# One layer's last weight pair: the sum of two weight tiles made by an accumulating DMA from GpSimd's queue instead of a VectorE add

## The chip, the cores and the metric

The kernel runs on one core of one Trainium2 chip. The metric is the device time of one execution in microseconds (us). A profiled execution also has a span, from its first to its last instruction, and a granted TensorE clock; both are given below.

## The reference

The program is a trunk of two layers over 512 tokens of width 2048, in float32. Each layer normalises its input, projects it once into all heads' columns, runs two groups of heads (a gated linear attention and a chunked attention), joins what they give, projects it once more, normalises that and adds it to the residual stream.

```python
def hybrid_layer(x, w_in, w_out, g_pre, g_post, ...):
    h = rmsnorm(x, g_pre)
    z = h @ w_in
    ...
    y = jnp.concatenate([o_gla, o_att], axis=-1) @ w_out
    return x + rmsnorm(y, g_post)

def reference(x, w_in, w_out, ...):
    h = x
    for l in range(DEPTH):
        h = hybrid_layer(h, w_in[l], w_out[l], ...)
    return h
```

The change lies in `... @ w_out`, in the half of its columns that the kernel computes last.

## The kernel before

**Precision.** Every float32 operand is split into a rounded part and a rest (ScalarE casts `wh`, VectorE subtracts to get `wl`), and a product is three matmuls: `wh` twice and `wl` once.

**Pairs.** Weight blocks are 512 columns wide. Most of them are taken in pairs by `fast_gemm`, which makes the eight block products of a 2x2 block multiplication from seven, P1 to P7, of sums and differences of weight blocks (this file makes them from loaded tiles as it goes) and of token blocks (made earlier, kept in DRAM, loaded again as `sa`). Each product has four steps c = 0 to 3, a step loads one or two weight tiles of 128 x 1024 (512 KB), and feeds 12 matmuls. A pair's products are listed in a fixed order: the last pair of a layer, `W23` (the last 1024 columns of `w_out`), has an order of its own, `PROD_END`:

```python
PROD_END = order("10 11 50 12 51 13 52 53 60 61 30 62 31 63 32 33 20 21 22 23 70 71 72 73 40 41 42 43")
```

"72" is step c = 2 of P7. So in the last pair the four steps of P2 come first, then the four of P7, and then the four of P4, after which the layer is over. `w_consume` takes the finished products: it adds two partial results on VectorE (`combine`, L318, into `t`), squares and scales them (L1086 on ScalarE, L1087 on VectorE).

**One job of the stream.** `Job.load` issues the DMAs on SyncE's queue (`fetch`, L140), `Job.high` makes the tile that is to be multiplied and its cast `wh` (L182, ScalarE), `Job.low` its rest `wl` (L186, VectorE). `ahead` keeps five loads, four highs and three lows in front of the job that is being multiplied (L356). Tiles live in rings: four buffers for `raw`, four for `H`, four for `wh`, three for `wl`. A DMA into a `raw` tile waits until the last reader of that buffer is done.

**P7 of the last pair.** It needs the sum of two tiles of the second weight block, rows `c + 4` and rows `c`. Here `load` fetches both, into two `raw` buffers, and `high` adds the second to the first on VectorE (L176 and L177), before the cast. So four steps of a layer take eight `raw` loads and four adds of 128 x 1024. In all other pairs P7 is a difference of `H` and one loaded tile (L179).

**What runs beside it.** Tasks are fed in between the products. In the last pair these are `finish_token` (L1098 to L1115: L1100 sums squares, L402 is a power on GpSimd that makes the factor, L1112 adds the residual on VectorE, then a store from GpSimd's queue) and, in the first layer, `prep_half` for the second layer: squares of the new rows (L415, ScalarE), their scaling (L455, VectorE), transposes on TensorE (L465), which ScalarE brings out of PSUM (L475) and splits with VectorE (L105 and L106, into tiles `a`, `g8` and others). The next layer's first product, L282, takes those. Its first two token tiles need the first half of `prep_half`; its last two need the second half, the tile `g8` first.

**Order.** The instruction order on each engine is made by a scheduler that runs with a timeline of its own when the kernel is built. Each engine then works through its list in order. In the last layer P4's last three steps are held back (`lag`), and after the last matmul come the last token tiles' sums, scaling and stores.

Of the kernel before, what the change touches and what calls it, by code (L numbers as in the profile page):

```python
# [11 lines left out]
ALU = mybir.AluOpType  # L12
# [21 lines left out]
def hybrid_trunk(  # L34
# [12 lines left out]
    nc = tc.nc  # L47
# [16 lines left out]
    def nm(s):  # L64
        serial[0] += 1
        return f"{s}_{serial[0]}"
# [4 lines left out]
    def rtile(tag, shape=(2, W), dtype=F32, bufs=4):  # L71
        return ring.tile([P] + list(shape), dtype, tag=tag, name=nm(tag), bufs=bufs)
# [28 lines left out]
    def flat(t):  # L101
        return t.bitcast(F32).rearrange("p a b -> p (a b)")
# [22 lines left out]
    W23 = (NB_IN + 2, NB_IN + 3)  # L125
# [8 lines left out]
    class Job:  # L134
# [8 lines left out]
        def load(self):  # L143
            k, c, p, b0, b1 = self.kind, self.c, self.pair, self.b0, self.b1
            end = b0 == W23[0]
            top, bottom = (c + 4, c) if end else (c, c + 4)
            if k == "std":
                self.raw = self.fetch(rtile("raw"), b0, c)
            elif k == "P1":
                p["H", c] = self.fetch(rtile("H"), b0, top)  # L150
            elif k == "P5":
                p["r", c] = self.fetch(rtile("raw"), b1, top)
            elif k == "P6":
                p["r", c] = self.fetch(rtile("raw"), b1, bottom)
            elif k == "P7" and end:
                p["r", c] = self.fetch(rtile("raw"), b1, top)
                p["r2", c] = self.fetch(rtile("raw"), b1, bottom)
            elif k == "P7":
                p["r", c] = self.fetch(rtile("raw"), b0, top)
            elif k == "P2":  # L160
                p["r", c] = self.fetch(rtile("raw"), b0, bottom)
            src = (so_d if end else sa_d)[self.l].get((LEFT.get(k), c))
            if src is not None:
                self.a = rtile("sa", (2, 512), F32R)
                nc.sync.dma_start(flat(self.a), src)

        def high(self):
            k, c, p = self.kind, self.c, self.pair
            if k == "std":
                src = self.raw  # L170
            else:
                h, r = p["H", c], p.get(("r", c))
                src = h if k in ("P1", "P5", "P6", "P4") else r
                if k in ("P5", "P6"):
                    nc.vector.tensor_tensor(out=h, in0=h, in1=r, op=ALU.add)  # L175
                elif k == "P7" and ("r2", c) in p:  # L176
                    nc.vector.tensor_tensor(out=r, in0=r, in1=p["r2", c], op=ALU.add)  # L177
                elif k == "P7":
                    nc.vector.tensor_tensor(out=r, in0=h, in1=r, op=ALU.subtract)  # L179
            self.src = src  # L180
            self.wh = rtile("wh", dtype=F32R)
            last_cast[0] = nc.scalar.copy(self.wh, src).ins  # L182
# [1029 lines left out]
```

## Time and profile before

| | |
|---|---|
| median of 3 runs | 1685.46 us (1684.21 to 1686.59) |
| the profiled execution's own time | 1684.26 us |
| its span | 1682.2 us |
| mean granted TensorE clock | 0.995 |
| PE busy | 1640.6 us, 98% |
| DVE busy | 1208.0 us, 72% |
| ACT busy | 873.8 us, 52% |
| POOL busy | 158.0 us, 9% |

PE is TensorE, DVE VectorE, ACT ScalarE, POOL GpSimd, SP SyncE; L12 is line 12 of the kernel. A group of the profile is written as line, engine, operation, the tile written, an arrow, the tiles read. Busy time is a sum over the whole span; the two places of the change (P7 of layer 0 from 813 us, of layer 1 from 1642 us) are some 17 us long each, so they hardly show in it, and have to be looked at in windows.

### The profile page before, as it was taken

Reading aid. Unit: us, or ns where it says so; the run is one execution under the profiler, and the core shown is the slowest. Engines: PE = TensorE matmul, PEld = TensorE weight load, DVE = VectorE, ACT = ScalarE, POOL = GpSimd, SP = SyncE. Lnnn points to the kernel's source line nnn. Section 1 sums busy time; section 2 is a strip of 40 time slices with the busy share of each in tenths; the row PEclk is TensorE's granted clock in tenths of the full one; section 3 lists DMA queues with packets and bytes.
Section 4 is the critical chain, followed back from the end, with each engine's and each line's share of the span. In section 5 each row is a group of like instructions: output and inputs, shape, how many; then the busy total and the mean of one; then the engine's idle time right before and its main releaser. Section 6 shows DMA issues by size and latency. Waiting matters only on the chain.

```text
span 1682.2 us, 24940 instructions
## 1 busy us (share of the span) xinstructions
PE 1640.6 (98%) x9090; PEld 1401.0 (83%) x9090; DVE 1208.0 (72%) x1563; ACT 873.8 (52%) x1460; POOL 158.0 (9%) x256
## 2 busy tenths in 40 slices
PE   7999999999999999999999999999999999999996
PEld 5888889999988887788778878899999888777884
DVE  5846767686876876568887567677777768764787
ACT  8634544456665554335684345444556655443443
POOL 0210100001100001210132000000001001012101
PEclk9999999999999999999999999999999999999998
DMA  7987987867858797589779788868587687865993
GB/s 255 368 300 232 345 273 251 278 223 254 300 175 302 241 354 253 174 316 322 253 251 364 248 291 288 326 210 305 174 309 255 206 284 256 335 218 193 351 342 146
DMA packets 143002, 455.04 MB, mean 271 GB/s; under 512 B 15444, under 2 KB 32212, under 8 KB 142880
## 3 DMA queue, kind: packets, MB, share of 16 engines
q1 hardware_dynamic: 119984, 373.76, 65.1%
q0 software_dynamic: 22176, 78.41, 12.0%
q8 instruction: 72, 1.18, 0.3%
q10 hardware_dynamic: 720, 1.28, 0.2%
q14 instruction: 50, 0.41, 0.1%
HBM read 381.28 MB, written 72.11 MB: 270 GB/s over the span
## 4 chain that ended last, share of the span: by engine, by line
PE 85%; issue 4%; DVE 4%; DMA 4%; POOL 1%; ACT 1%; SPq 0%; DVEq 0%; POOLq 0%; ACTq 0%
PE mm L356 40%; PE mm L346 18%; PE mm L282 16%; DMA raw<-in_w_dram 2%; PE ax L766 2%; DVE wl L186 1%; PE ax L356 1%; PE ax L920 1%; PE ax L954 1%; PE ax L604 1%; PE ax L749 1%; DMA sa<-S 1%; POOL sm L402 1%; PE ax L730 1%; PE ax L728 1%
## 5 line engine op out<-in xcount | busy, mean ns | idle before, releaser
L356 PE MATMUL mm<-wh,sa 128*128 128x512 f32 x1536 | 495.0, 394 | 3.1 <-DMA sa<-S 1.6
L182 ACT CAST wh<-raw 128x1024 fp32r<-128x1024 f32 x248 | 261.6, 1058 | 277.7 <-PE mm L356 84.6
L186 DVE TENSOR_TENSOR wl<-raw,wh 128x1024 fp32r<-128x1024 f32 x248 | 302.1, 1221 | 107.1 <-PE mm L356 37.0
L356 PEld LDWEIGHTS mm<-wh,sa 128*128 128x128 f32 x1536 | 289.6, 189 | 67.4 <-ACT wh L182 4.5
L182 ACT CAST wh<-H 128x1024 fp32r<-128x1024 f32 x224 | 234.2, 1051 | 196.6 <-PE mm L356 101.3
L186 DVE TENSOR_TENSOR wl<-H,wh 128x1024 fp32r<-128x1024 f32 x224 | 272.9, 1222 | 88.2 <-PE mm L356 37.9
L356 PE MATMUL mm<-wl,sa 128*128 128x512 f32 x768 | 301.2, 392 | 5.7 <-DVE wl L186 5.7
L346 PE MATMUL mm<-sa,wh 128*128 128x256 f32 x1280 | 236.5, 285 | 0.0
L346 PEld LDWEIGHTS mm<-sa,wh 128*128 128x128 f32 x1280 | 199.5, 191 | 0.1
L356 PE MATMUL mm<-wh,a 128*128 128x512 f32 x576 | 189.1, 393 | 1.9 <-DVE t L318 1.9
L346 PE MATMUL mm<-sa,wl 128*128 128x256 f32 x640 | 181.4, 284 | 0.6 <-DVE wl L186 0.6
L356 PEld LDWEIGHTS mm<-wl,sa 128*128 128x128 f32 x768 | 144.9, 189 | 35.6 <-DVE wl L186 6.7
L282 PE MATMUL mm<-wh,a 128*128 128x512 f32 x512 | 169.4, 395 | 4.0 <-ACT a L105 2.2
L175 DVE TENSOR_TENSOR H<-H,raw 128x1024 f32<-128x1024 f32 x112 | 136.3, 1222 | 9.5 <-DMA raw<-in_w_dram 8.0
L356 PEld LDWEIGHTS mm<-wh,a 128*128 128x128 f32 x576 | 107.9, 188 | 24.9 <-DVE t L318 2.2
L346 PEld LDWEIGHTS mm<-sa,wl 128*128 128x128 f32 x640 | 122.5, 191 | 0.9 <-DVE wl L186 0.8
L282 PEld LDWEIGHTS mm<-wh,a 128*128 128x128 f32 x512 | 95.9, 188 | 26.8 <-ACT a L105 3.0
L402 POOL TENSOR_TENSOR sm<-sm,mhalf 128x2 f32<-128x2 f32 (+2 forms) x44 | 51.1, 1162 | 698.1 <-DVE sm L776 469.7
L356 PE MATMUL mm<-wl,a 128*128 128x512 f32 x288 | 112.9, 392 | 0.0
L179 DVE TENSOR_TENSOR raw<-H,raw 128x1024 f32<-128x1024 f32 x48 | 58.8, 1225 | 62.4 <-DMA raw<-in_w_dram 62.3
L282 PE MATMUL mm<-wl,a 128*128 128x512 f32 x256 | 100.4, 392 | 0.1
L346 PE MATMUL mm<-a,wh 128*128 128x256 f32 x512 | 95.1, 285 | 0.0
(193 smaller groups left out, 2348.2 us busy)
## 6 DMA issues: line engine op xcount, KB each, us to landing
raw<-in_w_dram SPq DMA_DIRECT2D x312, 512.0 KB, 5.3
sa<-S SPq DMA_DIRECT2D x192, 512.0 KB, 4.7
H<-in_w_dram SPq DMA_DIRECT2D x56, 512.0 KB, 5.0
sa<-A SPq DMA_DIRECT2D x48, 512.0 KB, 6.2
S<-g POOLq DMA_DIRECT2D x32, 512.0 KB, 7.7
oS<-g POOLq DMA_DIRECT2D x32, 512.0 KB, 7.0
sa<-oS SPq DMA_DIRECT2D x32, 512.0 KB, 5.4
sg<-t POOLq DMA_DIRECT2D x32, 256.0 KB, 5.7
```

What stands on the lines that cost most here:

```text
L175: nc.vector.tensor_tensor(out=h, in0=h, in1=r, op=ALU.add)
L179: nc.vector.tensor_tensor(out=r, in0=h, in1=r, op=ALU.subtract)
L182: last_cast[0] = nc.scalar.copy(self.wh, src).ins
L186: nc.vector.tensor_tensor(out=self.wl, in0=self.src, in1=self.wh.bitcast(F32), op=ALU.subtract)
L282: nc.tensor.matmul(pss[o], a[:, part, t], rhs[:, kk, :], start=(i == 0 and kk == 0 and m == 0), stop=(i == n - 1 and kk == 1 and m == 2),)
L346: nc.tensor.matmul(dst, lhs[:, kk, f], a[:, part, tok], start=(fresh and kk == 0 and m == 0 and ft % 2 == 0), stop=(c == 3 and kk == 1 and ...
L356: nc.tensor.matmul(out_ps[t], a[:, part, tok], rhs[:, kk, :], start=(fresh and kk == 0 and m == 0), stop=(c == 3 and kk == 1 and m == 2), ...
L402: nc.gpsimd.tensor_tensor(out=out_r, in0=v, in1=mhalf[:, : v.shape[-1]], op=ALU.pow)
L604: nc.tensor.matmul(ps[0:96, half * 256 : (half + 1) * 256], wga[kt // 10][:, kt % 10, :], op[:, i, (kt % 2) * 256 : (kt % 2 + 1) * 256], s ...
L728: nc.tensor.matmul(ps[:, :n], self.qh[:, t], self.kh[:, :n], start=True, stop=False)
L730: nc.tensor.matmul(ps[:, :n], self.ql[:, t], self.kh[:, :n], start=False, stop=True)
L766: nc.tensor.matmul(o, self.pt[i][:, j * P : (j + 1) * P], av[hd // 4, j // 2][:, j % 2, (hd % 4) * P : (hd % 4 + 1) * P], start=(j == 0), ...
```

## The change

In `Job.load`, the second fetch of P7 in the last pair goes away. In its place GpSimd issues a DMA that adds rows `c` of the block in DRAM to the tile that SyncE has just fetched rows `c + 4` into. In `Job.high` the VectorE add goes away, and the cast reads the tile as it is. No other pair changes.

```diff
             elif k == "P7" and end:
                 p["r", c] = self.fetch(rtile("raw"), b1, top)
-                p["r2", c] = self.fetch(rtile("raw"), b1, bottom)
+                nc.gpsimd.dma_start(
+                    p["r", c], w[self.l, b1, bottom].rearrange("p (k n) -> p k n", k=2), accum_op=ALU.add
+                )
...
-                elif k == "P7" and ("r2", c) in p:
-                    nc.vector.tensor_tensor(out=r, in0=r, in1=p["r2", c], op=ALU.add)
-                elif k == "P7":
+                elif k == "P7" and self.b0 != W23[0]:
                     nc.vector.tensor_tensor(out=r, in0=h, in1=r, op=ALU.subtract)
```

Over the two layers SyncE's queue loses eight DMAs of 512 KB, VectorE eight adds of 128 x 1024, and GpSimd's queue gains eight DMAs of 512 KB. Since two lines are added in `load` and two taken away in `high`, lines from 178 on have the same numbers in both. The scheduler makes a new order for every engine.

On GpSimd in layer 0, between the last stores of the token sums (`oS`) and the first factor of `finish_token` (L402, `sm`), this stood before:

```order
L499 DMA oS403_139<-g3_1434_7391 128x1024
L402 TENSOR_TENSOR sm_1544_7910<-sm_1543_7909,mhalf_200 128x1
L1082 MEMSET ssy_2910_14855 128x1
L402 TENSOR_TENSOR sm_1548_7934<-sm_1547_7933,mhalf_200 128x1
L412 MEMSET sm_1553_7959 128x1
```

And now this; L157 is the accumulating DMA:

```order
L499 DMA oS403_139<-g3_1434_7391 128x1024
L157 DMA raw_1511_7792<-in_w_dram 128x1024
L157 DMA raw_1523_7828<-in_w_dram 128x1024
L157 DMA raw_1527_7849<-in_w_dram 128x1024
L157 DMA raw_1531_7870<-in_w_dram 128x1024
L402 TENSOR_TENSOR sm_1540_7902<-sm_1539_7901,mhalf_200 128x1
```

All four accumulating DMAs of the layer stand in a row, ahead of the factor; each of them waits for its own tile's first load from SyncE's queue. Layer 1 has the same four rows at the same place.

On VectorE in layer 0, from the end of P2 through the first three steps of P7, this stood before (`wl_1527`, `wl_1532` and `wl_1537` are the rests of P7's steps 0, 1 and 2; L318 with `ax` takes in P2's result):

```order
L1087 TENSOR_TENSOR g1_1518_7806<-t2_1517_7804,t2_1447_7466 128x512
L177 TENSOR_TENSOR raw_1511_7792<-raw_1511_7792,raw_1512_7794 128x1024
L186 TENSOR_TENSOR wl_1527_7848<-raw_1511_7792,wh_1523_7828 128x1024
L177 TENSOR_TENSOR raw_1524_7830<-raw_1524_7830,raw_1525_7832 128x1024
L318 TENSOR_TENSOR t2_1539_7899<-ax_1520_7810,ev_1474_7593 128x512
L1087 TENSOR_TENSOR g0_1515_7800<-t2_1539_7899,t2_1446_7464 128x512
L318 TENSOR_TENSOR t2_1541_7904<-ax_1521_7811,ev_1475_7595 128x512
L186 TENSOR_TENSOR wl_1532_7871<-raw_1524_7830,wh_1528_7851 128x1024
L177 TENSOR_TENSOR raw_1529_7853<-raw_1529_7853,raw_1530_7855 128x1024
```

And now this, with the rests of steps 0 to 3 named `wl_1525`, `wl_1529`, `wl_1533` and `wl_1541`:

```order
L1087 TENSOR_TENSOR g1_1517_7805<-t2_1516_7803,t2_1447_7466 128x512
L318 TENSOR_TENSOR t2_1535_7891<-ax_1519_7809,ev_1474_7593 128x512
L1087 TENSOR_TENSOR g0_1514_7799<-t2_1535_7891,t2_1446_7464 128x512
L186 TENSOR_TENSOR wl_1525_7845<-raw_1511_7792,wh_1522_7826 128x1024
L318 TENSOR_TENSOR t2_1537_7896<-ax_1520_7810,ev_1475_7595 128x512
L1100 TENSOR_REDUCE sm_1539_7901<-ssy_1351_7009 128x1
L1087 TENSOR_TENSOR g1_1517_7805<-t2_1537_7896,t2_1446_7464 128x512
L186 TENSOR_TENSOR wl_1529_7866<-raw_1523_7828,wh_1526_7847 128x1024
L1112 SCALAR_TENSOR_TENSOR g6_1369_7069<-g8_1352_7011,sm_1540_7902,g6_1369_7069 128x1024
L1112 SCALAR_TENSOR_TENSOR g7_1370_7070<-g0_1514_7799,sm_1540_7902,g7_1370_7070 128x1024
L1100 TENSOR_REDUCE sm_1543_7925<-ssy_1354_7021 128x1
L186 TENSOR_TENSOR wl_1533_7887<-raw_1527_7849,wh_1530_7868 128x1024
```

Besides the adds being gone, step 0's rest has moved behind the two operations that take in P2's result and so behind P2's end; after step 2's rest follow at once step 3's and that of P4's first step, and the second pair of L1112 comes after those. Layer 1 has the same order there.

On TensorE in layer 0, in P7's last step, transposes for layer 1 (L465) stood among the matmuls before (`sa_1536` is the token operand of P7's step 3, `g4_1329` that of P4's first step):

```order
L356 MATMUL mm_1449_7469<-wh_1538_7897,sa_1536_7880 128x512
L465 MATMUL ax_1561_7994<-cst_199,g6_1369_7069 128x128
L356 MATMUL mm_1450_7470<-wh_1546_7931,g4_1329_6915 128x512
L356 MATMUL mm_1451_7471<-wh_1546_7931,g4_1329_6915 128x512
L465 MATMUL ax_1564_8005<-cst_199,g7_1370_7070 128x128
L465 MATMUL ax_1577_8049<-cst_199,g6_1369_7069 128x128
```

Now the first of them stands at the very end of P4 (`g17_1288` is the token operand of P4's last step), and the next 31 lie between the last L356 and layer 1's first L282:

```order
L356 MATMUL mm_1451_7471<-wl_1581_8085,g17_1288_6692 128x512
L465 MATMUL ax_1557_7986<-cst_199,g6_1369_7069 128x128
L356 MATMUL mm_1451_7471<-wh_1563_8021,g17_1288_6692 128x512
L465 MATMUL ax_1560_7997<-cst_199,g7_1370_7070 128x128
L465 MATMUL ax_1573_8041<-cst_199,g6_1369_7069 128x128
```

All 32 transposes of the first half have moved from among P7 and P4 to behind them, ahead of layer 1's first matmul.

## The prediction

> **What bounds the kernel now.** I read the page first, then the groups of the added-tile line, the waits and the timelines around P7 in both layers, and stage windows.
>
> ```profile
> span 1682.2 us, 24940 instructions
> PE 1640.6 (98%) x9090; PEld 1401.0 (83%) x9090; DVE 1208.0 (72%) x1563; ACT 873.8 (52%) x1460; POOL 158.0 (9%) x256
> PE 85%; issue 4%; DVE 4%; DMA 4%; POOL 1%; ACT 1%; SPq 0%; DVEq 0%; POOLq 0%; ACTq 0%
> ```
>
> TensorE is busy for 98% of the span and carries 85% of the chain that ended last. A change pays only where TensorE stands still or runs at a lower clock. The groups of L177 and who waits for it:
>
> ```profile
> L177 DVE TENSOR_TENSOR raw<-raw,raw x8: 1218/1222/1226, 807.1 to 1653.3; 128x1024 f32<-128x1024 f32 x8
>   DMA raw<-in_w_dram: 0.8, 2
>   ACT wh L182: 17.7, 5
> ```
>
> Eight adds of 1.222 us, 9.8 us of VectorE in all, that hardly wait for their loads. ScalarE's casts wait 17.7 us for them, but ScalarE is at 52%. Does TensorE wait behind those casts? The timeline of TensorE in P7, layer 0 then layer 1 (start, duration; in brackets the wait before and its releaser):
>
> ```profile
> 813.26 0.62 PE L356 MATMUL mm<-wh,sa 128*128 128x512 f32 x2
> 813.71 0.39 PE L356 MATMUL mm<-wl,sa 128*128 128x512 f32 x1
> ...
> 821.88 0.50 PE L356 MATMUL mm<-wl,sa 128*128 128x512 f32 x1 [2.56 <-DVE wl L186]
> ...
> 831.29 0.39 PE L356 MATMUL mm<-wh,sa 128*128 128x512 f32 x1
> ```
> ```profile
> 1642.48 0.62 PE L356 MATMUL mm<-wh,sa 128*128 128x512 f32 x2
> ...
> 1647.69 0.84 PE L356 MATMUL mm<-wh,sa 128*128 128x512 f32 x3
> 1651.10 0.50 PE L356 MATMUL mm<-wl,sa 128*128 128x512 f32 x1 [2.57 <-DVE wl L186]
> ...
> 1659.57 0.39 PE L356 MATMUL mm<-wl,g 128*128 128x512 f32 x1
> ```
>
> Steps 0, 1 and the first two matmuls of step 2 run without a gap (26 starts from 1642.48 to 1648.14, one each 0.227 us, so 2.72 us for a step of 12). Then TensorE waits 2.56 us for step 2's rest. The windows show what follows (length, busy PE, PEld, DVE, ACT, POOL, then the granted clock and the DMA share):
>
> ```profile
> 818.91:822.32 3.41, 0.84 (x4) 0.40 (x3) 3.41 (x4) 2.29 (x4) 1.21 (x3) 1.00 0.73 286
> 822.32:825.73 3.41, 3.41 (x10) 2.43 (x8) 3.25 (x5) 2.57 (x5) 1.06 (x2) 0.50 0.99 315
> 20.19:23.60 3.41, 1.80 (x10) 1.27 (x9) 0.00 (x0) 3.41 (x11) 0.16 (x1) 1.00 0.64 235
> 23.60:27.01 3.41, 3.15 (x14) 2.62 (x15) 2.28 (x4) 3.41 (x7) 0.71 (x1) 1.00 0.00 0
> ```
>
> A window idle for 75% is followed by one at half clock, which costs another 1.7 us (half of 3.41); one idle for 47% was followed by full clock. The Trainium skill ("TensorE: Matmul & The Clock Gate", section on why this matters for your kernels) asks for no idle gap over some 3 us; here a gap of 2.56 us was already punished, so the trace is stricter, and by the page's rule the 1.7 us would not be there to win.
>
> **The change, VectorE's part.** VectorE works in order; layer 0 before:
>
> ```profile
> 812.78 0.69 DVE L318 TENSOR_TENSOR t<-ax,ev 128x512 f32<-128x512 f32 x1 [0.34 <-PE ax L356]
> 813.50 0.69 DVE L1087 TENSOR_TENSOR g<-t,t 128x512 f32<-128x512 f32 x1
> 814.12 0.68 DVE L318 TENSOR_TENSOR t<-ax,ev 128x512 f32<-128x512 f32 x1
> 814.72 1.22 DVE L186 TENSOR_TENSOR wl<-raw,wh 128x1024 fp32r<-128x1024 f32 x1
> 815.85 1.22 DVE L177 TENSOR_TENSOR raw<-raw,raw 128x1024 f32<-128x1024 f32 x1
> ...
> 818.21 2.48 DVE L1112 SCALAR_TENSOR_TENSOR g<-g,sm,g 128x1024 f32<-128x1024 f32 x2 [0.41 <-POOL ssy L1082]
> 820.60 1.22 DVE L186 TENSOR_TENSOR wl<-raw,wh 128x1024 fp32r<-128x1024 f32 x1
> ```
>
> The row at 820.60 is the rest that TensorE waited for. In the new order the add is gone, but step 0's rest stands behind L318 on P2's result, which cannot start before P2 ends. So a **new wait** is made: L318 at 812.78, L1087 at 813.50, step 0's rest from 814.12 to 815.34 (it was done long before 813.26), and TensorE's third matmul goes from 813.71 to 815.4: 1.7 us. Then L318, L1100, L1087, step 1's rest from 816.53 to 817.75 (wanted at 815.4 + 12 x 0.227 = 818.1: no wait), two L1112 to 820.1, step 2's rest until 821.36, wanted at 820.85: 0.5 us instead of 2.56, and step 3's, at once behind it, until 822.5: none. P7 ends at 821.4 + 22 x 0.227 = 826.4, with two early matmuls of P4 826.9, not 831.5 (831.29 + 0.23): 4.6 us earlier. The new gap of 1.7 us is at most 51% of a window, near the 47% that kept the clock, so I count no half clock, and 1.7 us a layer as its price if it comes.
>
> **Layer 1.** The same walk, 829.2 us later, gives 826.9 + 829.2 = 1656.1 for P4's remainder instead of 1659.57. Nothing but P4's matmuls and the closing token tiles stand behind it, so the **-3.4 us** reach the end.
>
> **Layer 0.** Here the 4.6 us run into layer 1's start. P4's other 46 matmuls end at 826.9 + 46 x 0.227 = 837.3, and only then come the 32 transposes. The tile that is late next is `g8`, the first of the second half, cast on ScalarE; its matmul, and ScalarE's groups from P4's new end until then:
>
> ```profile
> 874.15 0.50 PE L282 MATMUL mm<-wh,g 128*128 128x512 f32 x1
> ```
> ```profile
> L182 ACT CAST wh<-raw 128x1024 fp32r<-128x1024 f32 x11 | 11.7, 1073 | 5.0 <-DVE bias L1112 2.5 <-DMA raw<-in_w_dram 2.5
> L475 ACT ACTIVATE H<-ax,gcol 128x256 f32<-128x256 f32 x12 | 5.1, 545 | 0.0
> L105 ACT CAST a<-H 128x512 fp32r<-128x512 f32 x7 | 4.5, 697 | 0.0
> ```
>
> Between 837.2 and 874.1 ScalarE idles 5.0 us, so 31.9 of the 36.9 us are work. In the new order all 16 of the L475 stand behind P4 (12 did), all 8 casts of L105 (7 did), and a cast L182 and a half L475 pair more: 4 x 0.36 (545 ns less overlap) + 0.5 + 1.0 + 0.4 = 3.3 us. From 837.3 that is 872.5 without a wait and 877.5 with the same 5.0 us of waits: **-1.7 to +3.4 us** against 874.15. I take +1.5, nearer the upper end, because the waits on rows and loads have no reason to go, and the transposes (32 on one engine) come first.
>
> **The accumulating DMA.** No row of before has one. It starts when its tile's first load has landed and must be done before step 0's cast, 1.05 us ahead of its rest at 814.12. The loads, on SyncE's queue:
>
> ```profile
> 798.22 0.33 SPq L140 DMA_DIRECT2D raw<-in_w_dram  x1
> ...
> 800.94 0.33 SPq L140 DMA_DIRECT2D raw<-in_w_dram  x1
> ...
> 804.26 6.82 SPq L140 DMA_DIRECT2D raw<-in_w_dram  x4
> ```
> ```profile
> raw<-in_w_dram SPq DMA_DIRECT2D x312, 512.0 KB, 5.3
> S<-g POOLq DMA_DIRECT2D x32, 512.0 KB, 7.7
> ...
> g<-x_mid POOLq DMA_DIRECT2D x6, 512.0 KB, 4.7
> ```
>
> The four first loads keep the places of the first four issues (the last at about 806.6), and land at 803.5, 806.2, 809.6 and 811.9. So the accumulation has 9.5 us for step 0 (until 813.05), 9.3 for step 1 and about 9 for the others, hidden by P2's 48 matmuls. Bounds: 4.7 us, a plain load on that queue, and 15.4, twice its slowest row of this size. I take 9.4 us, twice the plain load, since each element has to be read from two places: late by 0.2 us in each layer, **+0.4**. Each microsecond more costs one in each layer, as VectorE is in order and the late rest blocks L318 and L1112 too.
>
> The Trainium skill ("Collectives: The Full Stack", why ReduceScatter is half of AllGather) says that an adding transfer is slow by its second source read and not by the adder. "DMA: Bandwidth & Descriptors" (anatomy of one DMA) fits 2.0 us + bytes / 436e3 for GpSimd's queue; doubled bytes would be an estimate of 4.4 us, inside the cover, which would make the term 0. No run shows it yet.
>
> Issuing four DMAs takes GpSimd a stretch in which it has nothing else (9% busy in the whole span); behind them queue L402 and the stores, which wait for L1100 behind L318 on P2's result, after step 3's first load has landed: nothing. SyncE's eight removed loads free places in the ring; every P7 load hardly waited (0.8 us), so nothing either; the bytes moved stay the same.
>
> **Sum.** -3.4 + 1.5 + 0.4 = -1.5 on the profiled execution's 1684.26 (span 1682.2 and 2.06 outside it): 1682.8. The median shown is 1.2 above that execution, so **1684.0**, by -0.09%: no change within 0.2%, which is about what a measurement of this kernel can tell.
>
> **Rivals.**
> 1. *Slower: the accumulation is later than its cover.* The point is about 10 us from issue to landing (0.95 us later in each layer would eat the 1.9). For it: DMA is 0.73 to 0.99 busy there, stores on this queue take 7.7, and twice that is 15.4. At 13 us each layer loses 3.7 us more, and the gap passes 75% of a window, so 1.7 of half clock: -1.9 + 7.4 + 3.4 = +8.9 over the sum without lateness's 0.4: 1694.4. At 15.4 us: 1699.
> 2. *Faster: ScalarE's chain closes up*, its waits shrinking as work is bunched: layer 0 at -1.7, total -5.1: 1680.4. Against it: two of the waits end at a DMA and at VectorE.
> 3. *Half clock at the new wait* (51% idle) and ScalarE at its upper end: -3.4 + 3.4 + 3.4 + 0.4 = +3.8: 1689.3. For it: two windows bracket the threshold between 47% and 75%.
> 4. That the adds are not removed is excluded by the orders: no L177 add is left, and SyncE has eight loads less.
>
> **Chances.** Forecast 0.40 (its own range 1681 to 1688), rival 1 0.38, rival 2 0.14, rival 3 0.08. Rival 1 reaches from 1686 upwards, a few hundredths of it lie within 0.2%, as a few hundredths of the forecast lie beyond. Faster by over 0.2%: 0.16; within: 0.40; slower: 0.44. Range 1679 to 1698: from rival 2's end to accumulations of about 15 us.
>
> **What would show it.** In the changed profile: in both layers the third matmul of P7 waits some 1.7 us for L186, the wait at step 2 is under 1 us, and no window is at half clock; L157 lands within 9.5 us of its issue; P4's remainder in layer 1 starts near 1656; the first `g8` matmul lies between 872 and 878. If the cast of step 0 waits for the DMA, rival 1 holds. I would be wrong altogether if the accumulation slowed other loads of that stage, or if SyncE's freed places shifted loads that TensorE waits for elsewhere.

## The result, and the profile after

The changed kernel is **slower by 0.27%**: ratio 1.0027, 95% interval 1.0016 to 1.0038, over 18 runs of each (medians 1691.53 and 1686.58 us). The profiled execution has a span of 1687.5 us, 5.3 more than before. The forecast was no change within 0.2%, at 1684.0 us.

The page of the changed kernel, its span, engines and chain:

```profile
span 1687.5 us, 24935 instructions
PE 1644.5 (97%) x9090; PEld 1403.2 (83%) x9090; DVE 1198.0 (71%) x1555; ACT 873.5 (52%) x1460; POOL 160.6 (10%) x264
PE 86%; issue 5%; DMA 3%; DVE 2%; POOL 1%; ACT 1%; SPq 0%; DVEq 0%; POOLq 0%; ACTq 0%
```

VectorE lost its 10 us, and its share of the chain fell from 4% to 2%. TensorE is still the bound, and its busy time rose by 3.9 us with the same 9090 matmuls: some of them ran at a lower clock. The group of the accumulating DMA, with who waited for it and its time from issue to landing:

```profile
L157 POOL DMA_DIRECT2D raw<-in_w_dram x8: 838/857/917, 806.5 to 1649.8; - x8
  ACT wh L182: 24.9, 8
DMA to landing us min/median/max: 5.6/8.2/10.6
```

The casts now wait 24.9 us for it, in all eight steps, where they waited 17.7 us for VectorE's add. P7 on TensorE, layer 0 (P2's last matmul ends at 815.03) and then layer 1 (1645.36); here and below a matmul's end is its start plus the 0.227 us that one takes at full clock:

```profile
815.88 0.73 PE L356 MATMUL mm<-wh,sa 128*128 128x512 f32 x2 [0.69 <-ACT wh L182]
817.16 0.50 PE L356 MATMUL mm<-wl,sa 128*128 128x512 f32 x1 [0.55 <-DVE wl L186]
...
820.45 0.50 PE L356 MATMUL mm<-wl,sa 128*128 128x512 f32 x1 [0.28 <-DVE wl L186]
...
826.36 1.22 PE L356 MATMUL mm<-wh,g 128*128 128x512 f32 x2 [2.88 <-ACT wh L182]
827.38 0.63 PE L356 MATMUL mm<-wl,sa 128*128 128x512 f32 x1
...
834.60 0.39 PE L356 MATMUL mm<-wh,sa 128*128 128x512 f32 x1
```
```profile
1646.79 0.73 PE L356 MATMUL mm<-wh,sa 128*128 128x512 f32 x2 [1.27 <-ACT wh L182]
1648.05 0.60 PE L356 MATMUL mm<-wl,sa 128*128 128x512 f32 x1 [0.53 <-DVE wl L186]
...
1657.51 0.73 PE L356 MATMUL mm<-wh,g 128*128 128x512 f32 x2 [2.13 <-ACT wh L182]
```

The old wait for step 2's rest is gone. In its place stands a wait of 2.88 and 2.13 us before two matmuls with token operand `g`: those are P4's first two, and in the new order they stand *ahead* of step 2's third matmul. They need the cast of P4's first weight tile. Where that cast stands shows on ScalarE:

```profile
824.32 1.04 ACT L182 CAST wh<-raw 128x1024 fp32r<-128x1024 f32 x1 [2.70 <-DMA raw<-in_w_dram]
825.27 1.04 ACT L182 CAST wh<-H 128x1024 fp32r<-128x1024 f32 x1
```

It stands behind step 3's cast (`wh<-raw`), which waits for the last accumulation, landed at 824.2. So TensorE waits in step 2 for step 3's transfer. And that one is late. The load of step 3 on SyncE's queue, the times to landing of the two such loads (layers 0 and 1), and the issues of layer 0's accumulations on GpSimd:

```profile
L140 SPq DMA_DIRECT2D raw<-in_w_dram x1: 333/333/333, 808.3 to 808.3; - x1
DMA to landing us min/median/max: 8.9/8.9/8.9
```
```profile
DMA to landing us min/median/max: 10.6/10.6/10.6
```
```profile
806.50 0.92 POOL L157 DMA_DIRECT2D raw<-in_w_dram  x1 [23.21 <-DVE wl L186]
809.05 0.86 POOL L157 DMA_DIRECT2D raw<-in_w_dram  x1 [1.63 <-DMA sa<-oS]
812.18 0.85 POOL L157 DMA_DIRECT2D raw<-in_w_dram  x1 [2.26 <-DMA raw<-in_w_dram]
817.89 0.84 POOL L157 DMA_DIRECT2D raw<-in_w_dram  x1 [4.86 <-DVE sm L1100]
```

Step 3's load, issued at 808.31, landed at 817.25; its accumulation went out at 817.89 and took 6.4 us. From load to sum that is 15.9 us in layer 0 and 16.8 in layer 1. (The wait at 817.89 is put down to L1100, which ended just before; the queue's own semaphore event shows that the load came last.) The clock, in windows of 3.41 us (in these profiles the granted clock changes only at whole multiples of this length; columns as in the prediction):

```profile
822.28:825.69 3.41, 1.21 (x6) 0.65 (x4) 2.00 (x4) 1.37 (x2) 1.67 (x6) 1.00 1.04 344
825.69:829.10 3.41, 2.74 (x7) 2.16 (x8) 3.41 (x4) 3.41 (x5) 0.00 (x0) 0.50 1.02 380
829.10:832.52 3.42, 3.42 (x10) 2.65 (x9) 2.17 (x3) 0.88 (x3) 1.10 (x2) 0.50 0.88 344
1644.89:1648.30 3.41, 1.61 (x6) 0.74 (x5) 2.90 (x4) 1.67 (x3) 0.85 (x1) 1.00 0.99 225
1648.30:1651.72 3.42, 3.42 (x9) 2.65 (x9) 2.18 (x4) 1.67 (x3) 1.89 (x2) 0.50 0.86 149
1655.13:1658.54 3.41, 1.28 (x6) 0.86 (x5) 2.78 (x3) 2.95 (x3) 1.20 (x2) 1.00 0.76 299
1658.54:1661.96 3.42, 3.42 (x10) 2.65 (x9) 2.90 (x4) 0.00 (x0) 0.84 (x2) 0.50 0.16 59
```

Each window at full clock that TensorE idled for 53% to 65% is followed by one at half clock: two such places in layer 1 where there was one. In layer 0 there is one such place as before, but two windows at half clock follow it, 825.69 and 829.10: the wait of 2.88 us reaches into the first of them, which TensorE idled for 20%. So each layer has one window at half clock more than before, by estimate 1.7 us (half of 3.41).

**Where the 5.3 us lie**, by TensorE's rows, counted from the end of P2's last matmul, so that what came before it drops out:

| | before | after | |
|---|---|---|---|
| layer 0: P7's last matmul ends | 18.25 | 19.79 | +1.5 |
| layer 0: layer 1's first matmul (L282) starts | 31.87 | 35.68 | +3.8 |
| layer 0: the 700th matmul behind P2's last ends | 155.40 | 159.15 | +3.8 |
| layer 1: P7's last matmul ends | 17.09 | 19.35 | +2.3 |
| layer 1: the last matmul of all ends | 27.51 | 29.78 | +2.3 |

3.8 + 2.3 = 6.1 us; the rest of the two executions differs by -0.8. Each column is one execution, and differences of about 1 us are within what a single one can show: in the run of experiment 6 that leaves layer 0 as it was, P7 of layer 0 took 19.26 us and not 18.25, and the 700th matmul came 1.0 us later, with the window at half clock in another place (829.24).

### The profile page after: what moved, and what is told of

It is laid out like the page before. It is cut to its first block, busy times and chain, and to the rows that moved or that the text cites. A ratio compares the mean times of both kernels' runs of the same rounds, so it can differ in the third digit from the quotient of the medians.

```text
span 1687.5 us, 24935 instructions
## 1 busy us (share of the span) xinstructions
PE 1644.5 (97%) x9090; PEld 1403.2 (83%) x9090; DVE 1198.0 (71%) x1555; ACT 873.5 (52%) x1460; POOL 160.6 (10%) x264
## 4 chain that ended last, share of the span: by engine, by line
PE 86%; issue 5%; DMA 3%; DVE 2%; POOL 1%; ACT 1%; SPq 0%; DVEq 0%; POOLq 0%; ACTq 0%
PE mm L356 41%; PE mm L346 19%; PE mm L282 16%; DMA raw<-in_w_dram 3%; PE ax L766 2%; PE ax L920 1%; PE ax L954 1%; PE ax L749 1%; DVE wl L186 1%; PE ax L604 1%; PE ax L730 1%; PE ax L728 1%; PE ax L729 1%; PE ax L791 0%; POOL oS L499 0%
## 5 line engine op out<-in xcount | busy, mean ns | idle before, releaser
L356 PE MATMUL mm<-wh,sa 128*128 128x512 f32 x1536 | 495.9, 395 | 2.2 <-ACT wh L182 2.0
L356 PEld LDWEIGHTS mm<-wh,sa 128*128 128x128 f32 x1536 | 290.9, 190 | 65.9 <-ACT wh L182 3.4
L356 PE MATMUL mm<-wl,sa 128*128 128x512 f32 x768 | 302.4, 394 | 1.4 <-DVE wl L186 1.3
L356 PE MATMUL mm<-wh,a 128*128 128x512 f32 x576 | 189.1, 393 | 1.9 <-DVE t L318 1.9
L282 PE MATMUL mm<-wh,a 128*128 128x512 f32 x512 | 169.7, 396 | 4.6 <-ACT a L105 2.2
L356 PEld LDWEIGHTS mm<-wl,sa 128*128 128x128 f32 x768 | 145.7, 190 | 32.5 <-DVE wl L186 3.2
L356 PEld LDWEIGHTS mm<-wh,a 128*128 128x128 f32 x576 | 107.9, 188 | 25.0 <-DVE t L318 2.2
L282 PEld LDWEIGHTS mm<-wh,a 128*128 128x128 f32 x512 | 95.7, 188 | 28.2 <-ACT a L105 3.1
L356 PE MATMUL mm<-wl,a 128*128 128x512 f32 x288 | 112.9, 392 | 0.0
L402 POOL TENSOR_TENSOR sm<-sm,mhalf 128x2 f32<-128x2 f32 (+2 forms) x44 | 47.2, 1072 | 644.3 <-DVE sm L776 471.0
L282 PE MATMUL mm<-wl,a 128*128 128x512 f32 x256 | 100.5, 392 | 0.0
```

The costliest lines, as they stand in the source:

```text
L282: nc.tensor.matmul(pss[o], a[:, part, t], rhs[:, kk, :], start=(i == 0 and kk == 0 and m == 0), stop=(i == n - 1 and kk == 1 and m == 2),)
L356: nc.tensor.matmul(out_ps[t], a[:, part, tok], rhs[:, kk, :], start=(fresh and kk == 0 and m == 0), stop=(c == 3 and kk == 1 and m == 2), ...
L402: nc.gpsimd.tensor_tensor(out=out_r, in0=v, in1=mhalf[:, : v.shape[-1]], op=ALU.pow)
```

## The experiments

P7's length below is taken in the same way, from the end of P2's last matmul to the end of P7's last, in layers 0 and 1. All ratios are against the kernel before.

**1. A copying second DMA**, in the changed kernel; the first term of the sum is left out.

```diff
-                    p["r", c], w[self.l, b1, bottom].rearrange("p (k n) -> p k n", k=2), accum_op=ALU.add
+                    p["r", c], w[self.l, b1, bottom].rearrange("p (k n) -> p k n", k=2)
```

> The changed kernel, with the second DMA of P7 copying over the first tile instead of adding to it (the first term of that weight sum is left out). Queue, waits and the order of instructions on all engines stay as in the changed kernel. Theory A (the adding itself makes the transfers slow and holds up the loads beside them): a copy lands some 5 us after its issue instead of 8.2 to 10.6 us, the load of step 3 lands in 5 to 6 us instead of 8.9 and 10.6 us, and the time falls by 3 to 5 us against the changed kernel, ratio to the kernel before 0.999 to 1.001. Rival B (it is the chain of two transfers, one after the other, whatever the second does): the same as the changed kernel, ratio 1.002 to 1.003, with landings of 8 us and more.

Ratio **0.9948** (0.9936 to 0.9960): not level with the kernel before but 9 us faster, beyond what theory A gave. The order is the same on VectorE, ScalarE and TensorE as in the changed kernel. The copying DMA's group, and the only wait in P7 of layer 0:

```profile
L157 POOL DMA_DIRECT2D raw<-in_w_dram x8: 537/541/545, 803.5 to 1639.1; - x8
DMA to landing us min/median/max: 3.6/5.3/7.2
```
```profile
814.67 0.50 PE L356 MATMUL mm<-wl,sa 128*128 128x512 f32 x1 [1.51 <-DVE wl L186]
```

P7 takes 13.3 us in both layers. Theory B falls: the chain of two transfers is kept, and does no harm when the second only copies. In stretches with hardly any load beside them, step 2's and 3's copies of layer 1 took 3.6 to 3.7 us, the adding ones 5.6; step 3's first load took 7.0 and 7.3 us here, 8.9 and 10.6 beside adding transfers. The DMA engines show the same; the queues in the stretch from 804 to 826 us, changed kernel and then this one (packets, MB, share of 16 engines):

```profile
q0 software_dynamic: 707, 2.62, 56.9%
q1 hardware_dynamic: 1093, 3.95, 47.9%
```
```profile
q1 hardware_dynamic: 1051, 3.83, 47.3%
q0 software_dynamic: 864, 3.15, 39.2%
```

GpSimd's queue (q0), its stores included, held the engines for 21.7% of the stretch per MB with adding transfers in it and 12.4% without: 1.75 times as much.

**2. P4's matmuls behind P7's**, in the changed kernel.

```diff
+                            with behind(last_p7[0] if end and k == "P4" else None):
                                 mm = nc.tensor.matmul(
...
+                            if k == "P7":
+                                last_p7[0] = mm.ins
```

Here `behind` is `tc.issue_after`, which keeps a matmul behind a given one in TensorE's list; in the changed kernel it moves the two early matmuls of P4 in each layer; besides, some operations of ScalarE and VectorE at the start of layer 1, from 846 us on, change places.

> The changed kernel, with P4's matmuls forced behind P7's last on TensorE; nothing else is moved up to there. In the changed kernel two of P4's matmuls stand ahead of the third matmul of P7's step 2, and wait for a cast that stands on ScalarE behind step 3's cast, which waits for the last accumulation. Theory C (this place in the order makes the long wait): the waits of 2.88 us and 2.13 us before P4's matmuls go, step 2 goes on when its own rest is there (some 3.4 and 2.1 us earlier), at least one window of half clock less in each layer, and the time falls by 3 to 6 us against the changed kernel: ratio 0.9990 to 1.0010. Rival D (the last accumulation is late for step 3 anyhow, and the wait only moves there): within 1 us of the changed kernel, ratio 1.002 to 1.003.

Ratio **0.9977** (0.9967 to 0.9988): faster than both kernels, by 8.4 us against the changed one. Theory C holds, more strongly than put; rival D falls. Layer 0's P7 in this run:

```profile
823.20 0.50 PE L362 MATMUL mm<-wl,sa 128*128 128x512 f32 x1 [0.58 <-DVE wl L187]
826.66 0.50 PE L362 MATMUL mm<-wl,sa 128*128 128x512 f32 x1 [0.43 <-DVE wl L187]
```

Step 2's rest is waited for 0.58 us and step 3's 0.43, though the accumulations are as slow as before (5.5/7.9/9.3 us to landing) and step 3's cast again starts at 824.3. P7 takes 14.8 and 15.0 us, with no half clock in either layer. The profiles agree with the ratios: against the changed kernel the 700th matmul comes 4.7 us earlier, and the last matmul of layer 1 3.9 us, 8.6 together.

**3. The same order on the kernel before**, VectorE's add kept.

> The kernel before, VectorE's add kept, with P4's matmuls forced behind P7's last as in the run that forced this for the changed kernel. Theory (before, the two early matmuls of P4 stood in step 3 and cost TensorE only waits of some 0.5 us, and the wait of 2.56 us for step 2's rest has another cause, VectorE's queue): ratio 0.9990 to 1.0010. Rival (the forced order is a gain by itself, and the accumulating DMA has no part in the 0.9977 of the run that forced it): ratio 0.9965 to 0.9985.

Ratio 1.0019 (1.0008 to 1.0030): a bit above the range expected, slower and not faster, so the rival falls. The forced order is no gain by itself. The wait for step 2's rest is untouched (and in layer 0 a second window at half clock follows, after two more waits of 1.30 and 0.52 us):

```profile
823.22 0.50 PE L362 MATMUL mm<-wl,sa 128*128 128x512 f32 x1 [2.56 <-DVE wl L187]
```

**4. Both: a copying DMA and the forced order.**

> The changed kernel with a copying second DMA instead of an adding one (the first term of the sum is left out) and P4's matmuls forced behind P7's last. Theory (with transfers as short as a copy's the place of P4's matmuls does not matter, since step 3's cast is early): ratio 0.9930 to 0.9965, as without the forced order (0.9948). The difference to the same order with adding transfers (0.9977) is then what the adding costs even in the better order: 2 to 7 us. Rival (order and transfers are two separate losses that add up): ratio 0.988 to 0.991.

Ratio 0.9956 (0.9942 to 0.9970), P7 13.3 us in both layers: the same as without the forced order, as the theory had it. The place of P4's matmuls costs something only because step 3's cast is late. Against the same order with adding transfers (0.9977), the adding still costs some 0.2%, 3.5 us by the two ratios, whose intervals just overlap.

**5. The queue alone**, in the kernel before: a plain load from GpSimd's queue, VectorE's add kept.

```diff
-                p["r2", c] = self.fetch(rtile("raw"), b1, bottom)
+                p["r2", c] = rtile("raw")
+                nc.gpsimd.dma_start(p["r2", c], w[self.l, b1, bottom].rearrange("p (k n) -> p k n", k=2))
```

> The kernel before, with only the queue of P7's second load changed: GpSimd issues it as a plain load into its own tile, and VectorE still adds. The order on all other engines is that of the kernel before. Theory (the queue alone costs nothing, what costs is that the second transfer waits for the first and shares the engines with it): ratio 0.999 to 1.001. Rival (GpSimd's queue brings data late by itself): the add L177 waits for its load where it waited 0.8 us in all, and the ratio is 1.001 to 1.003.

Ratio 1.0001 (0.9988 to 1.0013), the add waited 1.9 us for its loads in all, and they landed after 3.7/4.5/5.6 us. GpSimd's queue as such is not the cause.

**6. One layer at a time.**

```diff
-                p["r2", c] = self.fetch(rtile("raw"), b1, bottom)
+                if self.l == 1:
+                    nc.gpsimd.dma_start(
+                        p["r", c], w[self.l, b1, bottom].rearrange("p (k n) -> p k n", k=2), accum_op=ALU.add
+                    )
+                else:
+                    p["r2", c] = self.fetch(rtile("raw"), b1, bottom)
...
```

The other run has `self.l == 0` here.

> The accumulating DMA in layer 1 alone; layer 0 as before. Theory (each layer has its own loss, and layer 1's reaches the end undiminished, 2.3 us by the profile, while layer 0's is mostly taken up by the start of layer 1): ratio 1.0010 to 1.0020. Rival (the loss is made in layer 0, where the next layer stands behind it): ratio within 0.0005 of 1.

> The accumulating DMA in layer 0 alone; layer 1 as before. Theory (layer 0's loss, 3.8 us by the profiles' position in layer 1, stands by itself): ratio 1.0015 to 1.0030, as layer 1 alone measured 1.0003 against 1.0027 for both. Rival (each layer alone costs next to nothing, and the loss of 1.0027 is a matter of the clock's windows that differs from build to build): ratio 0.9995 to 1.0010.

Layer 1 alone: 1.0003 (0.9993 to 1.0012). Layer 0 alone: 1.0030 (1.0018 to 1.0041). So layer 0 carries the loss, as the second expectation had it, and the first was wrong in counting on 2.3 us from layer 1. With layer 0 alone the same wait stands in P7, longer still, and P7 takes 20.9 us:

```profile
828.11 1.22 PE L361 MATMUL mm<-wh,g 128*128 128x512 f32 x2 [4.74 <-ACT wh L187]
```

With layer 1 alone, its P7 took 17.06 us, just as before (17.09), and not 19.35, though TensorE waited even longer for P4's cast. The wait and the two windows over it:

```profile
1656.71 0.73 PE L361 MATMUL mm<-wh,g 128*128 128x512 f32 x2 [2.80 <-ACT wh L187]
```
```profile
1651.85:1655.26 3.41, 2.06 (x10) 1.35 (x8) 3.12 (x4) 0.70 (x2) 1.54 (x3) 1.00 0.79 231
1655.26:1658.67 3.41, 1.96 (x9) 1.62 (x10) 2.92 (x3) 2.36 (x3) 0.19 (x1) 1.00 0.41 163
```

The 2.80 us fell across two windows, 40% and 42% idle, and the clock stayed at 1.00. In the changed kernel's profile two waits fell each into one window. That accounts for the 2.3 us (two half windows would be 3.4), as far as one execution of each can show it.

**7. GpSimd's own add**, in the kernel before with the forced order; both loads are plain.

```diff
-                    nc.vector.tensor_tensor(out=r, in0=r, in1=p["r2", c], op=ALU.add)
+                    nc.gpsimd.tensor_tensor(out=r, in0=r, in1=p["r2", c], op=ALU.add)
```

> Both loads on SyncE's queue as before, the sum made by GpSimd's own add instead of VectorE's, and P4's matmuls forced behind P7's last. Theory (relieving VectorE pays when the sum is early and the transfers are plain): GpSimd's add of 128x512 took 1.735 us in the tail of the kernel before, so one of 128x1024 takes some 3.5 us and four in a row 14 us; the sums are ready at or before the accumulations' landings, loads take 4.5 to 5.8 us, and the ratio is 0.994 to 0.998. Rival (GpSimd's add is late, 3.5 us behind each pair of loads, or slows VectorE beside it): P7 waits over 2 us for its casts in each layer, ratio 0.998 to 1.002.

Ratio 1.0026 (1.0013 to 1.0039): slower, and a little above even the rival's range. GpSimd's add took 2.3 to 3.0 us and not 3.5, and step 1's cast was done in time, at 818.56. What TensorE waits for is step 1's rest. Rows of layer 0: GpSimd's adds of steps 1 and 2 with the factor L410 between them; step 1's cast; VectorE's pair of residual adds (L1120 here, L1112 in the kernel before), then the first of the pair alone, and step 1's rest behind them; and TensorE's wait for that rest, ahead of the third matmul of step 1:

```profile
814.34 3.01 POOL L178 TENSOR_TENSOR raw<-raw,raw 128x1024 f32<-128x1024 f32 x1 [1.59 <-DMA raw<-in_w_dram]
818.71 0.95 POOL L410 TENSOR_TENSOR sm<-sm,mhalf 128x1 f32<-128x1 f32 x1 [1.36 <-DVE sm L1108]
819.67 2.33 POOL L178 TENSOR_TENSOR raw<-raw,raw 128x1024 f32<-128x1024 f32 x1
```
```profile
817.52 1.04 ACT L183 CAST wh<-raw 128x1024 fp32r<-128x1024 f32 x1
```
```profile
819.70 4.59 DVE L1120 SCALAR_TENSOR_TENSOR g<-g,sm,g 128x1024 f32<-128x1024 f32 x2 [0.47 <-POOL ssy L1090]
819.70 3.39 DVE L1120 SCALAR_TENSOR_TENSOR g<-g,sm,g 128x1024 f32<-128x1024 f32 x1 [0.47 <-POOL ssy L1090]
824.21 1.21 DVE L187 TENSOR_TENSOR wl<-raw,wh 128x1024 fp32r<-128x1024 f32 x1
```
```profile
825.48 0.80 PE L362 MATMUL mm<-wl,sa 128*128 128x512 f32 x1 [5.49 <-DVE wl L187]
```

In this order step 1's rest stands behind the pair of residual adds; in the kernel before it stood ahead of them (814.72, the pair at 818.21). The pair runs beside GpSimd's add of step 2 and takes 4.59 us, where the kernel before took 2.48: the first of the two takes 3.39 us beside the add, the second, with the add over, 1.27. So of the wait of 5.49 us (5.46 in layer 1) some 2.1 come from VectorE being slowed, the rival's second mechanism, and the rest, by these rows, from the place of step 1's rest in the order. A late add, the rival's first mechanism, does not stand on this path. No run has GpSimd's add with step 1's rest ahead of the pair, so what the add costs by itself is not shown.

## Why the prediction was wrong, point by point

- **VectorE's part held.** With transfers in time (experiment 1) the new wait at step 0 was 1.51 us (forecast 1.7), step 2 waited not at all (0.5), and P7 in layer 1 ended 3.7 us earlier (forecast 3.4). In layer 0 it ended 4.9 us earlier (4.6).
- **The first accumulation was priced right.** It landed at 814.68; 803.5 + 9.4, moved by the 1.8 us between the two executions, is 814.7. The third matmul of P7 came 2.13 us after P2's end in layer 0 (forecast 815.4 - 813.26 = 2.14), and 2.69 in layer 1.
- **Layer 0's carry-over** was put at -1.7 to +3.4, and +1.5 taken. With transfers in time it is -2.7 us at the 700th matmul, beyond rival 2's end, and by rival 2's mechanism: between P4's last matmul and the first `g8` matmul ScalarE idled 2.6 us in experiment 1, where it idled 5.0 before. In the changed kernel itself it is +3.8, since P7 ended later, not earlier; from P7's end to the 700th matmul both kernels take 2.2 us more than the kernel before.
- **One step that failed is the landing times**: "land at 803.5, 806.2, 809.6 and 811.9". The first three loads of layer 0 came within 0.5 us of that (after the shift of 1.8 us between the executions). The last took 8.9 us instead of 5.3, and two loads of layer 1 took 9.1 and 10.6. I had priced the accumulation (9.4 us; measured 5.6 to 10.6) but not what it does to a load in flight beside it. The DMA rows of before had the engines at 0.73 to 0.99 busy there, and I used them for rival 1's chance only. That the accumulation could slow other loads stood among the signs of being wrong, without a term in the sum or a chance.
- **The other, and at the forecast's own price of an accumulation enough by itself, is the place of P4's first matmuls**, and with it the cover of step 3's accumulation, "about 9 for the others". The walk counted "two early matmuls of P4" as 0.45 us of work. I read them where they stood before, in step 3. In the new order they stand in step 2, behind a cast that is itself behind step 3's. By the walk's own times TensorE comes to them at 820.85, and the sum of step 3 is there at 811.9 + 9.4 = 821.3; with the two casts behind it (2.0 us by the rows of 824.32 and 825.27) that is an estimated wait of some 2.5 us in each layer, with every transfer as forecast. The cover was some 7 us. Experiment 2 shows that this place turned a late transfer into a loss: 8.4 us between the two orders.
- **Third, the clock.** "I count no half clock": a window 53% idle was followed by half clock in layer 1, and in layer 0 one at half clock, 20% idle, by another.
- **Rival 1** had the direction and the kind of loss (an accumulation later than its cover), but a wrong point of decision: not 10 us from an accumulation's issue, but the cover of some 7 us that this order leaves step 3, whose own accumulation took 6.4 us in layer 0, behind a load 3.6 us later than forecast. Its sign, step 0's cast waiting for the DMA, came true (6.9 us) and did not tell the two apart, as the third matmul was on time in layer 0 all the same. The prediction's own chances put slower (0.44) above within 0.2% (0.40); its forecast was not its likeliest outcome.

What stays open: why the copy gains 9 us by the ratio where its profile shows 2.7 + 3.7 = 6.4 us in the two layers (the interval begins at 6.7); how the 8.4 us between the two orders divide between the wait and the clock; and how the window's position falls over many runs, which only profiled executions show.

## What to carry to other kernels

A sum moved from an engine into a transfer has to be priced as a chain, load to sum, with its neighbours in flight: with adding transfers in it, GpSimd's queue held the DMA engines 1.75 times as long per byte, and the loads that lost most were issued beside them. When a wait becomes longer, look at what stands behind it on the same engine, and then at who stands behind that on the next one; two matmuls of 0.45 us, placed one step too early, were worth more than the whole change. With the order mended, the idea was good for 0.23% over the kernel before.

## What the runs showed of the hardware

- **In these profiles half clock goes by the idle share of a window, not by the length of a gap.** All ten profiles have changes of clock from which their windows of 3.41 us can be placed. Every window at full clock that TensorE idled for 61% or more was followed by half clock. Between 47% and 56% both happened (55% kept the clock in experiment 2, 53% lost it in the changed kernel); below 47% it was kept. A window at half clock that was idle for 20% or more was followed by another one (825.69 in the changed kernel), one idle for 6% or less by full clock. So a gap of 2.56 us in one window cost another 1.7 us by estimate, and one of 2.80 us over two windows cost none. The Trainium skill ("TensorE: Matmul & The Clock Gate", on why this matters for your kernels) advises against idle gaps over some 3 us, which is too mild for these runs.
- **An accumulating DMA of 512 KB** took 5.6 us from issue to landing with hardly any load beside it and 6.4 to 10.6 us with other transfers in flight (changed kernel), against 3.6 to 3.7 and up to 8.0 us for a copy on the same queue (experiments 1 and 4); its issue on GpSimd took 0.86 us against 0.54.
- **A GpSimd add beside VectorE** (128 x 1024, two inputs, 2.33 us): a residual add of VectorE that began 0.03 us behind it took 3.39 us, the next one, with the add over, 1.27 (experiment 7). The other way round, the GpSimd add of 814.34, which began while VectorE made a rest (813.87 to 815.09), took 3.01 us.
